# A two-layer attention and expert trunk on one core: the last norms behind the branch, four loads set apart, column sums by a product

## The chip, the core and the metric

The kernel runs on one core of a Trainium2 chip. The metric is the device time of one execution in microseconds. Five engines work side by side, each with its own queue of instructions that it takes in order: PE (TensorE, the matmuls), DVE (VectorE), ACT (ScalarE), POOL (GpSimd) and SP (SyncE, which issues nearly all loads). They wait for each other by semaphores.

## The reference

256 tokens of width 1024 go through two layers. Layer 0 mixes by multi-head latent attention (MLA), layer 1 by a sparse attention (DSA) with rotary keys, in which an indexer picks 64 keys for each query. After either mixer comes a PEER: eight heads, each with two sets of 128 keys, choose 16 of 16,384 experts for each token. Every sublayer ends in a norm. Cut to what matters here:

```
for i in range(2):
    m = _mla_mixer(x, ...) if i == 0 else _dsa_mixer(x, dsa_w_in, dsa_w_o)
    x = _layernorm(DN_ALPHA * x + m, ln_gain[i, 0], ln_bias[i, 0])
    f = _peer(x, peer_w_q[i], peer_sub_keys[i], peer_w_down[i], peer_w_up[i])
    x = _layernorm(DN_ALPHA * x + f, ln_gain[i, 1], ln_bias[i, 1])

def _peer(x, w_q, sub_keys, w_down, w_up):
    ...
    v1, i1 = lax.top_k(s1, 16)
    v2, i2 = lax.top_k(s2, 16)
    cand = (v1[..., :, None] + v2[..., None, :])          # 16 x 16 sums
    cand_idx = (i1[..., :, None] * 128 + i2[..., None, :])
    best, pos = lax.top_k(cand, 16)
    gate = softmax(best)
    a = einsum('td,ted->te', x, w_down[expert])
    y = einsum('te,ted->td', gelu(a) * gate, w_up[expert])
```

## The kernel before

**Number format.** PE multiplies in float16. Each f32 operand is split into two float16 parts, *hi* (ACT, line 88) and *lo* = value − hi (DVE, line 97; now and then POOL, lines 163 to 167, after ACT has scaled the raw block), and each product becomes three: hi·hi, hi·lo and lo·hi. Weights come in 512 KB blocks *raw* of 128 × 1024 (SP, line 132, six buffers), are split ahead of their use, and are multiplied by the tokens' parts *xh* and *xl*.

**The guard.** DVE's splits add up each lo as they go, one column of 128 partitions a split, in *sums*. At the end a judgement on these sums says whether float16 was safe: *fit* and *verdict* hold flags, `least` (line 559) squares the first 128 columns (*square*) and adds them over the partitions, `judge` (line 566) adds up the flags, and *sound* is their count. All engines load sound (line 1445) and compare it (line 1446); if a flag is missing, the whole computation is run a second time in a slower format (the fallback). Here it isn't: each engine goes past the fallback's code. `least` runs in the second PEER, whose code hands it to POOL between two of POOL's splits.

**The stages.** MLA, PEER, DSA, PEER. In the DSA, four pairs of query blocks (`heads(qT, h)`), then pairs of key blocks and the attention, head by head, and the output projection with w_o. Swapping halves for the rotation is two copies on ACT (lines 625 and 626), a product on POOL (627) and two operations on DVE (630 and 634); *s* are the scores. Four transfers of 512 KB for the norm behind the DSA (the layer's input x in two halves, gain and bias) are issued by SP in one go after the queries, lines 378, 611 and 612, ahead of the first w_o blocks.

A PEER has four parts: queries and scores; the down projection (products *d*, 64 steps of two key columns), during which the choice of experts is made; the placing of the gates (*gT*, *hot*, *place*, *G*); and the up projection (products *y*, 128 blocks). The choice (`choose`) is top-16 search on DVE (lines 1094 to 1098), then `pairs`: with the rank a of the first key only the first 16/(a + 1) of the second can be among the best 16, so 50 sums a head are made, in 16 adds on DVE (*cand*, line 1120) and 16 on POOL (*cell*, line 1123), for each of the two halves t of the tokens. The order in which the choice is mixed with the splits is set by a planner: each part yields its cost in ns, and `spend` takes as many parts as a step's income (PACE, 1420) pays for. Operations of one engine are then chained in this order.

`finish` ends a sublayer: the last four blocks of y for t = 0, then for t = 1, and the norms n0 and n1 (DVE lines 419 to 444, ACT 427, POOL 439). In the last layer it judges and stores the output (line 507); the branch comes behind it.

Of the kernel before, what the change touches and what calls it, by code (L numbers as in the profile page):

```python
# [10 lines left out]
F32 = mybir.dt.float32  # L11
# [4 lines left out]
ALU = mybir.AluOpType  # L16
# [23 lines left out]
OFF = [sum(SEG[:a]) for a in range(TOPK)]  # L40
CELLS = sum(SEG)
STAGGER = 4
PACE = 1420
# [21 lines left out]
BOTH, MOSTLY = 128, 704  # L65
CHECKS = 4 * P + BOTH

# [172 lines left out]
@with_exitstack  # L240
def tile_trunk(ctx: ExitStack, tc: tile.TileContext, ins, out: bass.AP, short, sound=None):
    nc = tc.nc
# [8 lines left out]
    rings = pool("rings", RING if short else 4)  # L251
    big = pool("big", 1)
    const = pool("const", 1)
# [3 lines left out]
    psp = pool("psp", 4, space=bass.MemoryType.PSUM)  # L257
    pyp = pool("pyp", 1, space=bass.MemoryType.PSUM)

# [6 lines left out]
    def py(i, name):  # L266
        return pyp.tile([P, 512], F32, tag=f"py{i}", name=name)
# [3 lines left out]
    fit = const.tile([P, 4], F32, tag="fit", name="fit")  # L271
    verdict = const.tile([1, 4 + BOTH], F32, tag="verdict", name="verdict")
    sound_rows = fit[:, 2:4]
    ones = lead.tile([P, 16], F32, tag="ones", name="ones")[:, 0:1]
    mhalf = lead.tile([P, 16], F32, tag="mhalf", name="mhalf")[:, 0:1]
    keep = [dram.tile([P, D], F32, tag=f"x{t}", name=f"x{t}") for t in range(2)]
# [7 lines left out]
    iotac = const.tile([P, CELLS, TOPK], F16, tag="iotac", name="iotac")  # L284
    arena = big.tile([P, 32768], F32, tag="arena", name="arena")
    A = arena.rearrange("p (b t) -> p b t", t=T)
# [11 lines left out]
    nc.vector.memset(mhalf, -0.5)  # L298

# [108 lines left out]
    class Norm:  # L408


        def __init__(self, queue, x, y2, g, b, r, z, sq):
            self.queue, self.x, self.y2, self.g, self.b, self.r, self.z, self.sq = queue, x, y2, g, b, r, z, sq
            self.st = small.tile([P, 6], F32, tag="st", name="st")

# [58 lines left out]
    def finish(y4, lhs_of, n, g, b, x, spare, lead=None):  # L473
# [21 lines left out]
        n0.result()  # L495
        if lead is None:
            if sound is not None:
                judge()
            n1.sums()
            n1.square()  # L500
            n1.centre()
            n1.scale()
            n1.result()
            for t in range(2):
                for h, q in enumerate((nc.sync, nc.scalar)):
                    s = slice(h * 512, (h + 1) * 512)
                    q.dma_start(out[t * P : (t + 1) * P, s], spare[t][:, s])
            return
        nc.sync.dma_start(keep[0], spare[0])
# [49 lines left out]
    def least():  # L559

        square = small.tile([P, BOTH], F32, tag="square", name="square", bufs=1)
        nc.gpsimd.tensor_tensor(square, split.cols[:, :BOTH], split.cols[:, :BOTH], op=ALU.mult)
        nc.gpsimd.tensor_reduce(square[0:1, :], square, axis=AX.C, op=ALU.add)
        nc.gpsimd.tensor_scalar(verdict[0:1, 4:], square[0:1, :], LEAST, None, op0=ALU.is_ge)

    def judge():

        assert not ws.late
        done = BOTH + split.n["most"]
        weigh_up(1, split.seen, done)  # L570
        nc.gpsimd.tensor_scalar(fit[:, 0:2], fit[:, 0:2], MOST * SMALL, None, op0=ALU.is_lt)  # L571
        nc.gpsimd.tensor_scalar(fit[:, 2:4], fit[:, 2:4], ROW, None, op0=ALU.is_ge)
        nc.gpsimd.tensor_reduce(verdict[0:1, 0:4], fit, axis=AX.C, op=ALU.add)
        nc.scalar.activation(verdict, verdict, AF.Copy, accum_out=fit[0:1, 0:1])
        nc.scalar.copy(sound, fit[0:1, 0:1])
# [358 lines left out]
    def dsa():  # L934
# [24 lines left out]
        proj(p[:72, :T], ws.get(), 72)  # L959
        xs, t1 = tmp()[:, 0, :], tmp()[:, 0, :]  # L960
        nc.scalar.copy(xs[0:32], p[32:64, :T])
        nc.scalar.copy(xs[32:64], p[0:32, :T])
# [3 lines left out]
        nc.scalar.copy(ki[64:128], ki[0:64])  # L966
        nc.scalar.mul(wT[64:72, :], p[64:72, :T], IDX_SCALE / unit)
        def weigh():
# [69 lines left out]
    def peer(li):  # L1038
# [74 lines left out]
        def pairs(t):  # L1113
            vh = v[t].rearrange("p (h two) k -> p h two k", two=2)
            dve(lambda: nc.vector.tensor_copy(idf[t], idx[t]))
            ih = idf[t].rearrange("p (h two) k -> p h two k", two=2)
            dve(lambda: nc.vector.tensor_scalar(ih[:, :, 0, :], ih[:, :, 0, :], float(NKEYS), None, op0=ALU.mult))
            for a in range(TOPK):
                w = slice(OFF[a], OFF[a] + SEG[a])
                dve(lambda: nc.vector.tensor_tensor(cand[t][:, :, w], vh[:, :, 1, 0 : SEG[a]],  # L1120
                                                    vh[:, :, 0, a : a + 1].to_broadcast([P, HEADS, SEG[a]]),
                                                    op=ALU.add))
                nc.gpsimd.tensor_tensor(cell[t][:, :, w], ih[:, :, 1, 0 : SEG[a]],
                                        ih[:, :, 0, a : a + 1].to_broadcast([P, HEADS, SEG[a]]), op=ALU.add)
# [162 lines left out]
        for k in range(NKEYS - STAGGER):  # L1287
            rows(y4, operand(k), ws.get(), k == 0, False)
            if k == 64:
                x = load_x(lnar, keep)  # L1290
                g, b = load_affine(lnar, li, 1)
                if last and sound is not None:
                    least()
# [3 lines left out]

        finish(y4, operand, NKEYS, g, b, x, spare, None if last else lead_values)

# [68 lines left out]
    dsa()  # L1368
    peer(1)

# [79 lines left out]
```

## Time and profile before

| | |
|---|---|
| median of 3 runs | 1746.27 us (1744.61 to 1748.59) |
| profiled execution, its own time | 1743.03 us |
| its span in the profile | 1741.7 us |
| mean granted TensorE clock | 0.994 |
| PE busy | 98% of the span |
| DVE, ACT, POOL busy | 78%, 63%, 24% |

In the profile a row of instructions gives the start and the duration in us, the engine, the line, the operation and what it writes and reads; behind it, in brackets, how long the engine had been idle and for whom it waited. A row of a window gives its ends and length, then each engine's busy time and count in the order PE, PEld (weight load), DVE, ACT, POOL, and then the granted TensorE clock, the share of the DMA engines and GB/s. A row of waits gives the total in us, how many times, and the longest. A row by line gives a count, the least, median and greatest duration in ns, and the first and last start.

### The profile page before, as it was taken

Reading aid. Unit: us, or ns where it says so; the run is one execution under the profiler, and the core shown is the slowest. Engines: PE = TensorE matmul, PEld = TensorE weight load, DVE = VectorE, ACT = ScalarE, POOL = GpSimd, SP = SyncE. Lnnn points to the kernel's source line nnn. Section 1 sums busy time; section 2 is a strip of 40 time slices with the busy share of each in tenths; the row PEclk is TensorE's granted clock in tenths of the full one; section 3 lists DMA queues with packets and bytes.
Section 4 is the critical chain, followed back from the end, with each engine's and each line's share of the span. In section 5 each row is a group of like instructions: output and inputs, shape, how many; then the busy total and the mean of one; then the engine's idle time right before and its main releaser. Section 6 shows DMA issues by size and latency. Waiting matters only on the chain.

```text
span 1741.7 us, 33230 instructions
## 1 busy us (share of the span) xinstructions
PE 1706.2 (98%) x12495; PEld 1195.2 (69%) x12495; DVE 1358.8 (78%) x3067; ACT 1095.5 (63%) x1905; POOL 418.8 (24%) x294
## 2 busy tenths in 40 slices
PE   9999999999999999999998999999999999999996
PEld 7678888999974444444676688889999944444443
DVE  7679999899986666665777899998899966666664
ACT  7665755888875455554667656567888855455552
POOL 3011354555530000000022143444555500000000
PEclk9999999999999999999999999999999999999999
DMA  9354556544466565555654435556444475565551
GB/s 343 139 182 170 206 182 212 207 174 172 170 211 225 204 206 201 203 202 204 222 190 159 169 145 188 196 198 219 171 171 176 174 245 205 204 205 203 200 204 50
DMA packets 93484, 335.62 MB, mean 193 GB/s; under 512 B 10368, under 2 KB 11392, under 8 KB 93312
## 3 DMA queue, kind: packets, MB, share of 16 engines
q1 hardware_dynamic: 93024, 332.87, 54.2%
q8 instruction: 100, 1.64, 0.4%
q14 instruction: 72, 0.59, 0.1%
q10 hardware_dynamic: 288, 0.52, 0.1%
HBM read 329.16 MB, written 4.19 MB: 191 GB/s over the span
## 4 chain that ended last, share of the span: by engine, by line
PE 78%; DVE 14%; issue 3%; DMA 2%; ACT 2%; POOL 1%; SPq 0%; POOLq 0%; DVEq 0%; ACTq 0%
PE y L341 40%; PE d L341 28%; DVE lo L97 6%; PE G L341 3%; DVE arena L1095 1%; DVE arena L1098 1%; DVE arena L1097 1%; PE qw L341 1%; DVE arena L1096 1%; ACT hi L88 1%; PE pq L341 1%; PE s L341 1%; DVE arena L1094 1%; PE q L341 1%; PE h L341 1%
## 5 line engine op out<-in xcount | busy, mean ns | idle before, releaser
L97 DVE SCALAR_TENSOR_TENSOR lo<-raw,hi 128x1024 f16<-128x1024 f32 (+1 forms) x571 | 784.0, 1377 | 229.5 <-ACT hi L88 228.6
L88 ACT ACTIVATE hi<-raw 128x1024 f16<-128x1024 f32 (+1 forms) x570 | 594.7, 1051 | 295.9 <-PE y L341 183.2
L341 PE MATMUL d<-xh,lo 128*128 128x256 f16 x2048 | 559.7, 273 | 8.1 <-DVE lo L97 5.7
L341 PE MATMUL d<-xh,hi 128*128 128x256 f16 x2048 | 560.0, 273 | 0.1
L341 PE MATMUL d<-xl,hi 128*128 128x256 f16 x2048 | 559.8, 273 | 0.0
L341 PEld LDWEIGHTS <-hi 128*128 128x128 f16 x5016 | 490.0, 98 | 60.2 <-issue 1.7
L341 PEld LDWEIGHTS <-xh 128*128 128x128 f16 x2320 | 226.4, 98 | 270.7 <-ACT xh L88 2.3
L341 PE MATMUL y<-lo,xh 128*128 128x512 f16 x1088 | 326.4, 379 | 0.0
L341 PE MATMUL y<-hi,xh 128*128 128x512 f16 x1088 | 326.0, 379 | 0.0
L341 PE MATMUL y<-hi,xl 128*128 128x512 f16 x1088 | 325.7, 379 | 0.0
L341 PEld LDWEIGHTS <-lo 128*128 128x128 f16 x2508 | 246.2, 98 | 40.8 <-DVE lo L97 8.4
L1218 POOL TENSOR_TENSOR gate<-hot,gate 128x512 f16<-128x512 f16 x128 | 219.8, 1736 | 191.6 <-DVE hot L1216 191.6
L341 PEld LDWEIGHTS <-xl 128*128 128x128 f16 x1160 | 113.3, 98 | 137.9 <-DVE xl L97 2.1
L1222 ACT ACTIVATE gate<-hot,rest 128x128 f16<-128x128 f16 x512 | 166.1, 413 | 5.3 <-DVE hot L1216 5.3
L88 ACT ACTIVATE xh<-arena 128x512 f16<-128x512 f32 x131 | 82.1, 629 | 133.3 <-PE y L341 132.3
L97 DVE SCALAR_TENSOR_TENSOR xl<-arena,xh 128x512 f16<-128x512 f32 x134 | 91.7, 687 | 60.4 <-ACT xh L88 60.2
L439 POOL TENSOR_TENSOR st<-st,mhalf 128x1 f32<-128x1 f32 x8 | 4.4, 555 | 422.0 <-DVE st L437 422.0
L167 POOL TENSOR_TENSOR lo<-raw,hi 128x1024 f16<-128x1024 f32 x26 | 58.7, 2260 | 175.1 <-ACT hi L165 141.5
L163 ACT ACTIVATE raw<-raw 128x1024 f32<-128x1024 f32 x26 | 27.5, 1056 | 112.2 <-DMA raw<-in_down 69.9
L1140 POOL TENSOR_TENSOR arena<-arena 128x800 f32<-128x800 f16 x32 | 73.9, 2308 | 77.0 <-DVE arena L1137 70.5
L1216 DVE TENSOR_TENSOR hot<-iota,place 128x1024 f16<-128x1024 f16 x128 | 82.8, 688 | 7.8 <-PE G L341 5.3
L571 POOL TENSOR_SCALAR fit<-fit 128x2 f32<-128x2 f32 x1 | 0.2, 228 | 326.3 <-DVE junk L556 326.3
(201 smaller groups left out, 1601.6 us busy)
## 6 DMA issues: line engine op xcount, KB each, us to landing
raw<-in_down SPq DMA_DIRECT2D x256, 512.0 KB, 3.3
raw<-in_up SPq DMA_DIRECT2D x256, 512.0 KB, 4.3
raw<-in_peer_q SPq DMA_DIRECT2D x24, 512.0 KB, 4.4
raw<-in_dsa_qk SPq DMA_DIRECT2D x16, 512.0 KB, 4.1
raw<-in_mla_w_o SPq DMA_DIRECT2D x8, 512.0 KB, 4.9
arena<-in_peer_q SPq DMA_DIRECT2D x8, 512.0 KB, 4.6
raw<-in_dsa_v SPq DMA_DIRECT2D x8, 512.0 KB, 4.5
raw<-in_dsa_w_o SPq DMA_DIRECT2D x8, 512.0 KB, 5.9
```

Of the source, the lines that this page charges most:

```text
L88: return nc.scalar.copy(o, src) if unit == 1.0 else nc.scalar.mul(o, src, unit)
L97: return nc.vector.scalar_tensor_tensor(o, src, unit, hi, op0=ALU.mult, op1=ALU.subtract, accum_out=total)
L163: self.act(lambda: nc.scalar.mul(raw, raw, unit))
L167: nc.gpsimd.tensor_tensor(lo, raw, hi if short else hi.bitcast(F32), op=ALU.subtract)
L341: return pe(lambda: nc.tensor.matmul(o, l, r, start=start, stop=stop, skip_group_check=True))
L1094: dve(lambda: nc.vector.max(vals[:, 0:8], src))
L1095: dve(lambda: nc.vector.max_index(ids[:, 0:8], vals[:, 0:8], src))
L1096: dve(lambda: nc.vector.match_replace(buf, vals[:, 0:8], src, GONE))
L1140: nc.gpsimd.tensor_tensor(o.rearrange("p k c -> p c k"), same, cell[t][:, h, :, None].to_broadcast([P, CELLS, TOPK]), op=ALU.mult)
L1216: nc.vector.tensor_tensor(hot, iota4[:, None].to_broadcast([P, 2, P, 4]), place16[:, :, None, four].to_broadcast([P, 2, P, 4]), op=ALU.is_ ...
L1218: nc.gpsimd.tensor_tensor(gate[:, 0], hot[:, 1].rearrange("p c j -> p j c"), gate16[:, four, None].to_broadcast([P, 4, P]), op=ALU.mult)
L1222: nc.scalar.mul(gate[:, 1, j, :], hot[:, 1, :, j], rest[:, t : t + 1])
```

## The change

1. `finish` for the last layer no longer makes the norms and the stores; it judges and returns a function `close` that makes them. The program calls it in the else arm of the condition, the fallback standing in the other arm. The pools that both arms need (the y banks, the arena, sound, mhalf, st) are made outside. The true arm, the fallback, stands straight behind the compare; the false arm stands behind it, and then the end of the program.
2. The DSA's four transfers are issued one at a time, each after one pair of query blocks.
3. `least` adds the squares over the partitions by one f32 product with a column of ones on PE, copies the 128 sums to a fifth column of fit on ACT, and compares there. A comparison of judge moves here too. verdict shrinks from 132 to 5 numbers, and the flags from 4 × 128 + 128 to 5 × 128.
4. `pairs` makes the sums of the ranks that have two partners in one add and those that have one in another: 7 adds on each engine for 16. It tells the planner 950 + 650 ns for 950 + 3 × 450.
5. In the DSA's `ki` a small scaling on ACT comes ahead of two copies.

```
-CHECKS = 4 * P + BOTH
+CHECKS = 5 * P
...
     def finish(y4, lhs_of, n, g, b, x, spare, lead=None):
...
-            norms.append(Norm(queue, x[t], y4[t], g, b, spare[t], spare[2 + t], spare[4]))
+            if lead is not None:
+                norms.append(Norm(queue, x[t], y4[t], g, b, spare[t], spare[2 + t], spare[4]))
+        if lead is None:
+            if short:
+                judge()
+
+            def close():
+                queue = queue_of()
+                for t in range(2):
+                    norm = Norm(queue, x[t], y4[t], g, b, spare[t], spare[2 + t], spare[4], shared["st"][t])
+                    norm.sums()
+                    norm.square()
+                    norm.centre()
+                    norm.scale()
+                    norm.result()
+                for t in range(2):
+                    for h, q in enumerate((nc.sync, nc.scalar)):
+                        s = slice(h * 512, (h + 1) * 512)
+                        q.dma_start(out[t * P : (t + 1) * P, s], spare[t][:, s])
+
+            return close
...
     def least():
         square = small.tile([P, BOTH], F32, tag="square", name="square", bufs=1)
+        p = ps("least")
         nc.gpsimd.tensor_tensor(square, split.cols[:, :BOTH], split.cols[:, :BOTH], op=ALU.mult)
-        nc.gpsimd.tensor_reduce(square[0:1, :], square, axis=AX.C, op=ALU.add)
-        nc.gpsimd.tensor_scalar(verdict[0:1, 4:], square[0:1, :], LEAST, None, op0=ALU.is_ge)
+        mm(p[:, 0:1], square, ones, True, True)
+        nc.scalar.copy(fit[:, 4:5], p[:, 0:1])
+        nc.gpsimd.tensor_scalar(fit[:, 4:5], fit[:, 4:5], LEAST, None, op0=ALU.is_ge)
+        nc.gpsimd.tensor_scalar(fit[:, 2:4], fit[:, 2:4], ROW, None, op0=ALU.is_ge)
...
+        x, g, b = [ar.take(D), ar.take(D)], ar.take(D), ar.take(D)
+        aside = [(x[0], keep[0]), (x[1], keep[1]), (g, ins["ln_gain"][1, 0].partition_broadcast(P)),
+                 (b, ins["ln_bias"][1, 0].partition_broadcast(P))]
         for h in range(0, HEADS, 2):
             turn_all(heads(qT, h))
+            with tc.issue_after(ws.last):
+                nc.sync.dma_start(*aside.pop(0))
         ws.share = 0
-        with tc.issue_after(ws.last):
-            x = load_x(ar, keep)
-            g, b = load_affine(ar, 1, 0)
...
-            for a in range(TOPK):
...
-                if a % 4 == 3:
-                    yield (950, 450, 450, 450)[a // 4]
...
+            for a in range(TWOS):
+                both(a, SEG[a], lambda i: i[:, :, 1, 0 : SEG[a]],
+                     lambda i: i[:, :, 0, a : a + 1].to_broadcast([P, HEADS, SEG[a]]))
+                if a == 3:
+                    yield 950
+            n = ONES - TWOS
+            both(TWOS, 2 * n, ...)
+            both(ONES, TOPK - ONES, ...)
+            yield 650
...
+        close = tile_trunk(tc, aps, o, True, shared)
+        count = nc.values_load(shared["sound"], min_val=0, max_val=CHECKS, ...)
+        with tc.If(count < CHECKS) as unsound:
+            tile_trunk(tc, aps, o, False, shared)()
+        with unsound.Else():
+            close()
```

How it moves instructions is shown at three places. First POOL in the second PEER, before; lo with raw and hi is a split:

```order
L167 TENSOR_TENSOR lo_11422<-raw_11218,hi_11421 128x1024 [waits PE_49,Activation_49,Pool_49]
L562 TENSOR_TENSOR square<-sums 128x128 [waits DVE_49]
L563 TENSOR_REDUCE square<-square 1x128 [waits Pool_49]
L167 TENSOR_TENSOR lo_11585<-raw_11387,hi_11584 128x1024 [waits PE_49,Activation_49]
L167 TENSOR_TENSOR lo_11748<-raw_11550,hi_11747 128x1024 [waits PE_49,Activation_49]
L564 TENSOR_SCALAR verdict<-square 1x128 [waits Pool_49]
```

and in the change:

```order
L168 TENSOR_TENSOR lo_11387<-raw_11183,hi_11386 128x1024 [waits PE_49,Activation_49,Pool_49]
L569 TENSOR_TENSOR square<-sums 128x128 [waits DVE_49]
L168 TENSOR_TENSOR lo_11550<-raw_11352,hi_11549 128x1024 [waits PE_49,Activation_49]
L168 TENSOR_TENSOR lo_11713<-raw_11515,hi_11712 128x1024 [waits PE_49,Activation_49,Pool_49]
L168 TENSOR_TENSOR lo_11859<-raw_11673,hi_11858 128x1024 [waits DVE_49,PE_49,Activation_49]
```

The reduction and the comparison behind it have gone from between the splits; the product that takes their place stands on PE at the end of d.

Then SP in the DSA, from the last blocks of queries and keys (in_dsa_qk) to the first of w_o, before (x is the layer's input, in two halves):

```order
L132 DMA raw_10268<-in_dsa_qk 128x1024 [waits Pool_49]
L132 DMA raw_10304<-in_dsa_qk 128x1024 [waits DMAHW7_49,DVE_49]
L132 DMA raw_10335<-in_dsa_qk 128x1024 [waits DMAHW6_49,DMAHW0_49,DVE_49]
L132 DMA raw_10372<-in_dsa_qk 128x1024 [waits Pool_49]
L132 DMA raw_10402<-in_dsa_qk 128x1024 [waits DMAHW2_49,DVE_49]
L378 DMA arena<-x_97 128x1024 [waits DMAHW1_49,PE_49]
L378 DMA arena<-x_98 128x1024 [waits PE_49]
L611 DMA arena<-in_ln_gain 128x1024 [waits DMAHW3_49,PE_49]
L612 DMA arena<-in_ln_bias 128x1024 [waits DMAHW4_49]
L132 DMA raw_10442<-in_dsa_w_o 128x1024 [waits DMAHW5_49,DVE_49]
L132 DMA raw_10473<-in_dsa_w_o 128x1024 [waits DMAHW6_49,DVE_49]
```

and in the change:

```order
L1032 DMA arena<-x_98 128x1024 [waits PE_49]
L133 DMA raw_10204<-in_dsa_qk 128x1024 [waits DMAHW5_49,DVE_49]
L133 DMA raw_10234<-in_dsa_qk 128x1024 [waits Pool_49]
L1032 DMA arena<-x_99 128x1024 [waits DMAHW6_49,PE_49]
L133 DMA raw_10271<-in_dsa_qk 128x1024 [waits DMAHW7_49,DVE_49]
L133 DMA raw_10302<-in_dsa_qk 128x1024 [waits DMAHW0_49,DVE_49]
L1032 DMA arena<-in_ln_gain 128x1024 [waits DMAHW1_49,PE_49]
L133 DMA raw_10340<-in_dsa_qk 128x1024 [waits DMAHW2_49,Pool_49]
L133 DMA raw_10370<-in_dsa_qk 128x1024 [waits DMAHW3_49,DVE_49]
L1032 DMA arena<-in_ln_bias 128x1024 [waits DMAHW4_49]
L133 DMA raw_10407<-in_dsa_w_o 128x1024 [waits DMAHW5_49,DVE_49]
L133 DMA raw_10438<-in_dsa_w_o 128x1024 [waits DMAHW6_49,DVE_49]
```

Three of the four transfers have moved ahead by six, four and two blocks of in_dsa_qk, and one alone still stands before w_o.

Last, ACT at the same place. raw_10473 is the second w_o block, which POOL splits, and q_10437 the first pair of key blocks, before:

```order
L88 ACTIVATE hi_10505<-raw_10335 128x1024 [waits DMAHW6_49,PE_49]
L625 COPY arena<-q_10366 64x512 [waits DVE_49,PE_49]
L626 COPY arena<-q_10366 64x512 [waits Activation_49]
L88 ACTIVATE hi_10535<-raw_10372 128x1024 [waits DMAHW7_49,PE_49]
L163 ACTIVATE raw_10473<-raw_10473 128x1024 [waits DMAHW6_49,DVE_49]
L88 ACTIVATE hi_10599<-raw_10402 128x1024 [waits DMAHW0_49,PE_49]
L625 COPY arena<-q_10437 64x512 [waits DVE_49,PE_49]
L626 COPY arena<-q_10437 64x512 [waits Activation_49]
```

and in the change, where they are raw_10438 and q_10402:

```order
L89 ACTIVATE hi_10433<-raw_10271 128x1024 [waits DMAHW7_49,PE_49]
L164 ACTIVATE raw_10438<-raw_10438 128x1024 [waits DMAHW6_49,DVE_49]
L89 ACTIVATE hi_10470<-raw_10302 128x1024 [waits DMAHW0_49,PE_49]
L633 COPY arena<-q_10334 64x512 [waits PE_49,Pool_49]
L634 COPY arena<-q_10334 64x512
L89 ACTIVATE hi_10500<-raw_10340 128x1024 [waits DMAHW2_49,PE_49]
L89 ACTIVATE hi_10564<-raw_10370 128x1024 [waits DMAHW3_49,PE_49]
L633 COPY arena<-q_10402 64x512 [waits DVE_49,PE_49]
L634 COPY arena<-q_10402 64x512 [waits Activation_49]
```

The scaling of the second w_o block has moved ahead of two hi and a pair of copies.

More of the change, by code (lines that the diff above doesn't have):

```diff
@@ L240, in tile_trunk @@
 @with_exitstack
-def tile_trunk(ctx: ExitStack, tc: tile.TileContext, ins, out: bass.AP, short, sound=None):
+def tile_trunk(ctx: ExitStack, tc: tile.TileContext, ins, out: bass.AP, short, shared):
     nc = tc.nc
@@ L257, in tile_trunk @@
     psp = pool("psp", 4, space=bass.MemoryType.PSUM)
-    pyp = pool("pyp", 1, space=bass.MemoryType.PSUM)
+    pyp, arena, mhalf, sound = shared["pyp"], shared["arena"], shared["mhalf"], shared["sound"]
     def oh_tile(tag, dt=F32):
@@ L408, in tile_trunk, with __init__ @@
     class Norm:
[L411 removed]
+        def __init__(self, queue, x, y2, g, b, r, z, sq, st=None):
             self.queue, self.x, self.y2, self.g, self.b, self.r, self.z, self.sq = queue, x, y2, g, b, r, z, sq
[L413 removed]
+            self.st = small.tile([P, 6], F32, tag="st", name="st") if st is None else st
         def sums(self):
@@ L495, in finish @@
         n0.result()
[L496 to L508, printed above, removed]
         nc.sync.dma_start(keep[0], spare[0])
@@ L1117, in pairs, with both @@
             dve(lambda: nc.vector.tensor_scalar(ih[:, :, 0, :], ih[:, :, 0, :], float(NKEYS), None, op0=ALU.mult))
-            for a in range(TOPK):
[L1119 to L1124, printed above, removed]
-                if a % 4 == 3:
-                    yield (950, 450, 450, 450)[a // 4]
+            def both(w, n, first, second):
+                k = OFF[w]
+                for engine, o, i in ((nc.vector, cand[t], vh), (nc.gpsimd, cell[t], ih)):
+                    o, f, g = o[:, :, k : k + n], first(i), second(i)
+                    if len(f.shape) == 4:
+                        o = o.rearrange("p h (a b) -> p h a b", b=f.shape[3])
+                    if engine is nc.vector:
+                        dve(lambda: engine.tensor_tensor(o, f, g, op=ALU.add))
+                    else:
+                        engine.tensor_tensor(o, f, g, op=ALU.add)
+            for a in range(TWOS):
[4 more added lines that the diff above has]
+            n = ONES - TWOS
+            both(TWOS, 2 * n, lambda i: i[:, :, 1, None, 0:2].to_broadcast([P, HEADS, n, 2]),
+                 lambda i: i[:, :, 0, TWOS:ONES, None].to_broadcast([P, HEADS, n, 2]))
+            both(ONES, TOPK - ONES, lambda i: i[:, :, 0, ONES:TOPK],
+                 lambda i: i[:, :, 1, 0:1].to_broadcast([P, HEADS, TOPK - ONES]))
+            yield 650
             for h in range(HEADS):
@@ L1291, in peer @@
                 g, b = load_affine(lnar, li, 1)
-                if last and sound is not None:
+                if last and short:
                     least()
@@ L1296, in peer @@
         spare = [lnar.take(D) for _ in range(5)]
-        finish(y4, operand, NKEYS, g, b, x, spare, None if last else lead_values)
+        return finish(y4, operand, NKEYS, g, b, x, spare, None if last else lead_values)
     xt = Arena(arena, 30720).take(NC, T)
@@ L1368, in tile_trunk @@
     dsa()
-    peer(1)
+    return peer(1)
 def _blocks(w):
@@ L1440 @@
     o = nc.dram_tensor("out_y", (T, D), F32, kind="ExternalOutput").ap()
-    with tile.TileContext(nc, schedule_with_timeline_sim=True) as tc:
-        with tc.tile_pool(name="sound", bufs=1) as pool:
-            sound = pool.tile([1, 1], mybir.dt.int32, tag="sound", name="sound")
-            tile_trunk(tc, aps, o, True, sound)
-            count = nc.values_load(sound, min_val=0, max_val=CHECKS, skip_runtime_bounds_check_because="it counts CHECKS flags")
-            with tc.If(count < CHECKS, preferred_fallthrough_block=False):
-                tile_trunk(tc, aps, o, False)
+    with tile.TileContext(nc, schedule_with_timeline_sim=True) as tc, ExitStack() as ctx:
+        held = ctx.enter_context(tc.tile_pool(name="held", bufs=1))
+        shared = {
+            "pyp": ctx.enter_context(tc.tile_pool(name="pyp", bufs=1, space=bass.MemoryType.PSUM)),
+            "banks": {},
+            "sound": held.tile([1, 1], mybir.dt.int32, tag="sound", name="sound"),
+            "st": [held.tile([P, 6], F32, tag=f"end{t}", name=f"end{t}") for t in range(2)],
+            "mhalf": held.tile([P, 16], F32, tag="mhalf", name="mhalf")[:, 0:1],
+            "arena": held.tile([P, 32768], F32, tag="arena", name="arena"),
+        }
+        nc.vector.memset(shared["mhalf"], -0.5)
+        close = tile_trunk(tc, aps, o, True, shared)
+        count = nc.values_load(shared["sound"], min_val=0, max_val=CHECKS,
+                               skip_runtime_bounds_check_because="it counts CHECKS flags")
+        with tc.If(count < CHECKS) as unsound:
+            tile_trunk(tc, aps, o, False, shared)()
+        with unsound.Else():
+            close()
     r = run_bass_kernel_spmd(nc, [arrays], core_ids=[0])
```

18 lines of the change are left out of this document (8 added, 10 removed).

## The prediction

> **What bounds the kernel now.** I read the page's head and chain first, then what PE waits for, then windows over the stages that the change touches.
>
> ```profile
> PE 1706.2 (98%) x12495; PEld 1195.2 (69%) x12495; DVE 1358.8 (78%) x3067; ACT 1095.5 (63%) x1905; POOL 418.8 (24%) x294
> PE 78%; DVE 14%; issue 3%; DMA 2%; ACT 2%; POOL 1%; SPq 0%; POOLq 0%; DVEq 0%; ACTq 0%
> PE s L341 <- DVE arena L634: 5.8, 1, 5.8
> PE d L341 <- DVE lo L97: 5.7, 4, 3.9
> 142.00:265.00 123.00, 122.79 (x1126) 109.92 (x1125) 116.10 (x411) 78.14 (x101) 44.99 (x48) 1.00 0.53 188
> 985.00:1140.00 155.00, 146.98 (x1316) 129.71 (x1314) 143.35 (x474) 89.39 (x118) 61.79 (x52) 0.99 0.46 167
> ```
>
> PE is the bound, and the change leaves its matmuls alone but for one. So it can only win where PE stands still or is clocked down, and after PE's last matmul. The two wait rows (total, times, longest) name the two places: one stall of 5.8 us at the DSA's first scores, and splits (lo) that come late in the second PEER. The two windows are the same stage, queries and choice, of the first PEER and the second: with DVE busy for 94% of it the first loses 0.21 us of PE, the second 8.02.
>
> **The lanes' reduction (L563).** What the second PEER has and the first has not:
>
> ```profile
> 1009.47 14.37 POOL L563 CROSS_LANE_REDUCE square<-square 128x128 f32<-128x128 f32 x1
> 1023.83 4.19 POOL L167 TENSOR_TENSOR lo<-raw,hi 128x1024 f16<-128x1024 f32 x2
> 1010.42 5.65 DVE L97 SCALAR_TENSOR_TENSOR lo<-raw,hi 128x1024 f16<-128x1024 f32 x1
> 1019.14 2.70 DVE L97 SCALAR_TENSOR_TENSOR lo<-raw,hi 128x1024 f16<-128x1024 f32 x1
> 1023.35 5.75 DVE L97 SCALAR_TENSOR_TENSOR lo<-raw,hi 128x1024 f16<-128x1024 f32 x1
> 1030.62 1.21 DVE L97 SCALAR_TENSOR_TENSOR lo<-raw,hi 128x1024 f16<-128x1024 f32 x1
> 1025.00:1030.00 5.00, 1.10 (x11) 0.75 (x9) 4.94 (x7) 0.00 (x0) 4.50 (x3) 1.00 0.00 0
> 1030.00:1035.00 5.00, 5.00 (x33) 3.85 (x31) 4.75 (x22) 0.00 (x0) 0.00 (x0) 0.66 0.69 253
> 1035.00:1040.00 5.00, 5.00 (x48) 4.49 (x46) 4.06 (x18) 4.75 (x7) 0.00 (x0) 1.00 0.27 81
> 1140.00:1145.00 5.00, 5.00 (x36) 4.01 (x34) 4.84 (x19) 4.21 (x7) 2.13 (x1) 0.74 0.83 315
> ```
>
> While POOL reduces, and then makes the two splits that stood behind it, three splits of DVE take 14.1 us where three at 1.21 take 3.63: 10.5 us of DVE gone. PE then has nothing for 3.90 us of 1025:1030, and runs at a granted clock of 0.66 in the next 5 us (33 matmuls, where 48 go at full clock: 1.56 us lost). DVE, at 92% in this stage, hardly makes that up. The remaining waits of the stage follow, and a second clocked stretch (36 of 48, 1.25 us) behind them.
>
> The edit takes L563 and L564 away and gives POOL two small operations on 128 partitions instead. If the backlog is the cause of all stalls of this stage, 8.02 + 1.56 + 1.25 = 10.8 us go, less what the first PEER loses at the same rate (0.21/123 × 155 = 0.3): **−10.5**. If only the stall straight behind it goes, −(3.90 + 1.56) = −5.5. I take −10.5: the first PEER is the nearest measurement, being the same code without the reduction.
>
> **The sums of pairs, 16 to 7 on each engine, twice in a PEER.**
>
> ```profile
> 1078.95 3.17 DVE L1120 TENSOR_TENSOR arena<-arena 128x128 f32<-128x128 f32 x16
> 1132.74 3.22 POOL L1123 TENSOR_TENSOR arena<-arena 128x128 f32<-128x128 f32 x16 [3.54 <-DVE arena L1117]
> 1135.91 2.13 POOL L167 TENSOR_TENSOR lo<-raw,hi 128x1024 f16<-128x1024 f32 x1
> 1135.00:1140.00 5.00, 2.70 (x20) 1.79 (x19) 4.79 (x21) 5.00 (x8) 3.04 (x7) 0.92 0.00 0
> ```
>
> Nine of 16 adds less are 9/16 × 3.2 = 1.8 us of each engine, four times. On DVE that is cover, not path, once the backlog is gone: 0. On POOL it brings the split at 1135.91 forward, for which PE stood 2.30 us; that stall is counted above already. With the reduction gone the adds' saving makes sure of it; so this part is at 0 beside the −10.5, and −2.3 without it. The lower charge of the planner moves the choice ahead against the splits, but by the order no split of DVE in either PEER gets more DVE work in front of it than it had, since nine adds have gone: 0, bounds ±1.
>
> **The product in place of the reduction.** One f32 matmul with its load stands where the second PEER turns from d to y.
>
> ```profile
> L341 PEld LDWEIGHTS ms<-ones,arena x8: 190/192/193, 27.8 to 36.8; 128*128 128x128 f32 x8
> L341 PE MATMUL ms<-ones,arena x8: 169/250/251, 27.9 to 36.8; 128*128 128x1 f32 x8
> ```
>
> The same shape costs 0.25 us, 0.44 with its load uncovered: **+0.3**. Its operand is ready long before. The copy on ACT lies beside PE: 0.
>
> **The four loads of the DSA.**
>
> ```profile
> 904.68 1.06 ACT L88 ACTIVATE hi<-raw 128x1024 f16<-128x1024 f32 x1 [0.35 <-PE q L341]
> 913.12 1.06 ACT L163 ACTIVATE raw<-raw 128x1024 f32<-128x1024 f32 x1 [7.38 <-DMA raw<-in_dsa_w_o]
> 915.75 0.58 ACT L626 COPY arena<-q 64x512 f32<-64x512 f32 x1
> 916.40 1.27 POOL L627 TENSOR_TENSOR arena<-arena 128x512 f32<-128x512 f32 x1 [10.02 <-ACT arena L626]
> 917.70 0.69 DVE L634 TENSOR_TENSOR arena<-arena 128x512 f32<-128x512 f32 x1 [0.66 <-POOL arena L627]
> 905.28 0.33 SPq L132 DMA_DIRECT2D raw<-in_dsa_w_o  x1
> raw<-in_dsa_w_o SPq DMA_DIRECT2D x4, 512.0 KB, 6.8
> raw<-in_dsa_qk SPq DMA_DIRECT2D x3, 512.0 KB, 3.6
> 915.00:920.00 5.00, 1.55 (x5) 1.37 (x6) 2.99 (x5) 4.87 (x8) 1.65 (x2) 0.74 0.00 0
> 920.00:925.00 5.00, 5.00 (x27) 3.68 (x26) 4.93 (x16) 2.70 (x9) 3.89 (x2) 0.58 0.57 211
> ```
>
> The scores wait for the first keys: ACT's swap copies, POOL, DVE in a chain, and ACT stood in front of them until the second w_o block had landed. Four loads of 512 KB ahead of it made it take 6.8 us instead of the 3.6 of a dsa_qk block. Spread out they are done sooner: on SP each now stands between two dsa_qk loads, where SP waits for buffers anyway; an issue takes 0.33 us like the one shown, and what the loads overwrite has been free since the first layer: 0 for what is queued behind them. It is still issued at 905.28 (by the lo that frees its buffer), so by the 3.6 it lands about 908.9 instead of 912 to 913. But in the new order ACT meets it two blocks earlier, and ahead of the keys' copies stand, from 908.9: the scaling 1.06, three hi of 1.05, two pairs of copies of 1.2, together 6.6, so 915.5. Before, the copies ended at 916.33: **−0.8**. A landing at 3.1 us would make it −1.3, one as late as before 0 to +2.4. The clock stays at 0.58 to 0.74 for two stretches here, so it takes a shorter stall to save one of them: the windows give 1.7 us for it at most, which I keep for the range.
>
> The Trainium skill's page "TensorE: Matmul & The Clock Gate" (Part 1, "What's actually happening") has full clock return after one busy window of 3.4 us in a grid that runs free of the kernel. The trace's first slow window holds 1.1 us of idle, so its second slow one agrees; by that rule a chance shift of the grid alone could make this part −2.5.
>
> **The end.** Norms and stores behind the branch instead of ahead of it:
>
> ```profile
> 1716.93 0.19 ACT L575 CAST sound<-fit 1x1 int32<-1x1 f32 x1
> 1722.41 0.69 DVE L419 SCALAR_TENSOR_TENSOR arena<-arena,y 128x512 f32<-128x512 f32 x1 [7.03 <-PE y L341]
> 1727.59 0.69 DVE L419 SCALAR_TENSOR_TENSOR arena<-arena,y 128x512 f32<-128x512 f32 x1
> L1445 DVEq TENSOR_LOAD <-sound x1: 541/541/541, 1731.4 to 1731.4; - x1
> L1446 DVEq COMPARE_BRANCH  x2: 51/58/65, 1732.0 to 1732.9; - x2
> L1441 DVEq DRAIN  x2: 10/34/58, 1736.6 to 1740.3; - x2
> L1446 SPq COMPARE_BRANCH  x2: 38/46/53, 1733.1 to 1736.7; - x2
> L1441 SPq EVENT_SEMAPHORE  x10: 17/28/28, 1739.4 to 1741.6; - x10
> ```
>
> Now SP waits for the last store to land (1736.7), takes the branch over the fallback, and goes on at 1739.4: 2.7 us on the path. In the change each engine branches as soon as sound is written, and the end lies straight behind the arm. So these 2.7 go, **−2.7** (2.5 to 3.2 with the semaphore checks that follow). The price is a jump ahead of the norms: on DVE 3.65 us (1732.95 to 1736.6). From sound at 1717.12 come the load, 0.54, the compare, 0.06, and the jump: 1721.4. DVE isn't wanted before 1722.41, so 1.0 us is left over. n1's sums (1727.59) begin without idle time behind n0, so each microsecond of excess would be lost whole. SP, ACT and POOL are wanted only after DVE's first sums.
>
> **Sum.** −10.5 + 0.3 − 0.8 − 2.7 = −13.7. The profiled execution took 1743.03 us (a span of 1741.7), which is 0.19% under the median of the runs, 1746.27; on that median it makes 1732.6, and I say **1732**.
>
> **Rivals.**
> - *Only the stall straight behind the reduction goes.* DVE at 92% of the stage is for it, the first PEER at 94% without a stall is against it. −5.5 + 0.3 − 0.8 − 2.7 = −8.7: 1737.5. Chance 0.16.
> - *The jump doesn't fit into DVE's wait.* The arm's code has to be brought in twice, say at a block border: another 3.7 (DVE's own jump). n0 then begins at 1725.1, 2.7 late, and the end gains nothing: 1735. For it speaks that the jumps in the trace take some 50 times their compares; against it the 1 us left. Chance 0.12. The Trainium skill's page "Runtime: NRT & Kernel Launch" (Instruction fetch mechanics) says that a taken branch out of a window of two pages fetches the target's page before it goes on; the jumps of 2.5 to 3.65 us agree, and no run here shows a second fetch.
> - *Slower: the choice, drawn forward by the lower charge, crowds out the splits in both PEERs.* DVE's lead there is worth about 6.6 us (10.5 lost, 3.90 felt by PE); if more work than that comes before a split, the first PEER too pays 10.8 and the second keeps its own: +10.8 + 0.3 − 0.8 − 2.7 = +7.6, 1754. Against it stands the order. Chance 0.04.
> - *The work that the reduction hid was not the backlog's cause, and the end's wait comes back elsewhere*, so that no part shows: within 0.2% (about 3.5 us, what the runs can tell). Chance 0.05.
>
> The forecast itself (1728 to 1734) has 0.63. The range takes in the first two rivals, and below the clock's 1.7 and the DSA's 0.5: 1726 to 1740. Faster 0.91, same 0.05, slower 0.04.
>
> **What would show it.** No POOL row of 14 us at 1009, DVE's splits there at 1.2, PE busy for over 154 of 155 us in that stage, and a granted clock of 1.00 from 1030 to 1150. L163 of the second w_o block runs about 909, the scores start about 917.6. DVE's first sums of the end start when y is ready, no more than 0.1 after it, and SP's last wait runs straight into the end. I am wrong if PE stalls for lo still near 1080 and 1135 of the old time, if DVE reaches the arm later than y, or if ACT's early wait for w_o starves the splits behind it.

## The result, and the profile after

The changed kernel takes 1729.91 us (median of 4 runs, 1728.14 to 1732.27) against 1746.13: a ratio of 0.9907, with a 95% interval of 0.9889 to 0.9924. That is 16.2 us less, where 14 were forecast. Its profiled execution took 1731.02 us, with a span of 1729.1. One execution of run 1 below took 2221.39 us at a granted clock of 0.753; it stands in that run's median, not in its ratio.

First the same views as before: the page's head and chain, PE's waits, and the windows over the two PEERs' queries and choice, moved with the work (1.5 us later in the first, 3 us later in the second).

```profile
PE 1702.9 (98%) x12497; PEld 1193.2 (69%) x12497; DVE 1346.9 (78%) x3033; ACT 1096.5 (63%) x1908; POOL 393.5 (23%) x257
PE 86%; DVE 7%; issue 3%; ACT 2%; DMA 1%; POOL 1%; DVEq 0%; SPq 0%; POOLq 0%; ACTq 0%
PE s L340 <- DVE arena L642: 4.6, 1, 4.6
PE d L340 <- DVE lo L98: 2.4, 3, 1.0
PE G L340 <- POOL gate L1242: 1.8, 4, 0.5
143.50:266.50 123.00, 120.86 (x1102) 107.28 (x1101) 115.67 (x393) 75.39 (x99) 39.74 (x30) 1.00 0.54 181
988.00:1143.00 155.00, 154.12 (x1406) 137.72 (x1404) 139.20 (x505) 96.83 (x127) 45.51 (x33) 1.00 0.56 182
1028.00:1033.00 5.00, 5.00 (x49) 4.49 (x47) 4.72 (x22) 4.97 (x9) 0.00 (x0) 1.00 0.46 161
1138.00:1143.00 5.00, 4.99 (x46) 4.24 (x45) 4.79 (x21) 4.58 (x6) 0.36 (x1) 1.00 0.52 184
```

DVE has halved its share of the chain, from 14% to 7%. The second PEER loses 0.88 us of PE where it lost 8.02, and both stretches of half clock there are gone (the granted clock is 1.00 from 1030 to 1150). But the first PEER, which lost 0.21, now loses 2.14, and the scores' stall is down by only 1.2 us. New are the waits of G for POOL's gates: two in each PEER, 1.8 us together.

Since PE does the same matmuls in both, the trace can be cut at the first matmul of each kind. The table gives the us from cut to cut; the last column is the range over the profiles of other kernels below whose code in that stage is the changed kernel's.

| stage | before | after | other profiles |
|---|---|---|---|
| first PEER, first d to first y | 365.66 | 369.39 | 366.9 to 368.1 |
| DSA, first q to first scores | 37.46 | 36.22 | 36.2 to 37.7 |
| scores to the second PEER's queries | 55.05 | 53.99 | 53.9 to 55.8 |
| second PEER, first d to first y | 377.98 | 368.40 | 366.6 to 368.6 |
| last y to the end of the span | 13.84 | 7.96 | 7.9 to 8.0 |

All other stages agree within 0.6 us, or 1 at the start. Ahead of the first d these add up to 1.5 us, by which profiles of one code differ there too (142.4 to 143.9). On the means of these profiles the change is worth about +1.9 in the first PEER (367.7 against 365.8), −1 in the DSA, −10.1 in the second PEER (367.9), and −5.6 at the end (two more profiles with the end as before have 13.3 and 13.5). That makes −14.8, inside the interval of the ratio (−13 to −19). So the sum of the forecast holds, and several of its terms do not.

At the place of the reduction, POOL and the splits of DVE:

```profile
1012.08 0.40 POOL L569 TENSOR_TENSOR square<-sums 128x128 f32<-128x128 f32 x1 [12.45 <-PE pq L340]
1012.43 2.13 POOL L168 TENSOR_TENSOR lo<-raw,hi 128x1024 f16<-128x1024 f32 x1
1021.92 2.71 POOL L168 TENSOR_TENSOR lo<-raw,hi 128x1024 f16<-128x1024 f32 x1 [7.36 <-ACT hi L166]
L98 DVE SCALAR_TENSOR_TENSOR lo<-raw,hi x8: 1204/1206/2144, 1010.8 to 1035.8; 128x1024 f16<-128x1024 f32 x8
```

POOL goes straight on to its split, and the eight splits of DVE from 1011 to 1036 have a median of 1.21 us; only those beside a split of POOL take longer (2.14).

The DSA, ACT's and POOL's rows ahead of the scores and the DMA rows of w_o from 895 to 915:

```profile
913.89 1.06 ACT L164 ACTIVATE raw<-raw 128x1024 f32<-128x1024 f32 x1 [8.15 <-DMA raw<-in_dsa_w_o]
915.92 0.58 ACT L633 COPY arena<-q 64x512 f32<-64x512 f32 x1
919.75 0.58 ACT L634 COPY arena<-q 64x512 f32<-64x512 f32 x1
920.41 1.27 POOL L635 TENSOR_TENSOR arena<-arena 128x512 f32<-128x512 f32 x1 [1.96 <-ACT arena L634]
raw<-in_dsa_w_o SPq DMA_DIRECT2D x3, 512.0 KB, 3.6
```

The second w_o block now lands about 4 us after its issue. Yet ACT waits longer for it, 8.15 us for 7.38, as it comes to it earlier; behind it stand a hi, the copies at 915.92, two more hi and only then the keys' copies, ending at 920.33. First q is at 886.24 here and at 880.99 before, so the copies end 34.1 us after it where they ended after 35.3.

The end, ACT's sound, DVE's first sums, the branch, SP's checks, and the stores:

```profile
1710.30 0.19 ACT L583 CAST sound<-fit 1x1 int32<-1x1 f32 x1
1715.85 0.69 DVE L418 SCALAR_TENSOR_TENSOR arena<-arena,y 128x512 f32<-128x512 f32 x1 [7.09 <-PE y L340]
L1479 DVEq COMPARE_BRANCH  x1: 76/76/76, 1711.1 to 1711.1; - x1
L1479 SPq COMPARE_BRANCH  x1: 54/54/54, 1711.1 to 1711.1; - x1
L1465 SPq EVENT_SEMAPHORE  x12: 17/28/28, 1714.3 to 1729.1; - x12
DMA to landing us min/median/max: 2.0/2.1/2.4
```

The jump fits: DVE starts when y is ready, 5.34 us ahead of the last matmul's start as against 5.41. The stores land in 2.0 to 2.4 us. In the kernel before the same row, and the instruction fetches from the first store to the end (packets, MB, share), read:

```profile
DMA to landing us min/median/max: 2.1/3.0/3.9
q14 instruction: 8, 0.07, 1.4%
q8 instruction: 2, 0.03, 1.1%
```

and in the changed kernel, whose jumps lie ahead of the stores, but for PE's, the fetches are:

```profile
q8 instruction: 2, 0.03, 1.3%
```

### The profile page after: what moved, and what is told of

It reads as the page before. It is cut to its first block, busy times and chain, and to the rows that moved or that the text cites. A ratio compares the mean times of both kernels' runs of the same rounds, so it can differ in the third digit from the quotient of the medians.

```text
span 1729.1 us, 33166 instructions
## 1 busy us (share of the span) xinstructions
PE 1702.9 (98%) x12497; PEld 1193.2 (69%) x12497; DVE 1346.9 (78%) x3033; ACT 1096.5 (63%) x1908; POOL 393.5 (23%) x257
## 4 chain that ended last, share of the span: by engine, by line
PE 86%; DVE 7%; issue 3%; ACT 2%; DMA 1%; POOL 1%; DVEq 0%; SPq 0%; POOLq 0%; ACTq 0%
PE y L340 40%; PE d L340 33%; PE G L340 3%; DVE lo L98 2%; PE pq L340 2%; PE qw L340 1%; ACT hi L89 1%; PE v L340 1%; PE s L340 1%; PE o L340 1%; PE h L340 1%; DMA raw<-in_down 1%; PE ps L340 1%; PE q L340 1%; PE qi L340 1%
## 5 line engine op out<-in xcount | busy, mean ns | idle before, releaser
L98 DVE SCALAR_TENSOR_TENSOR lo<-raw,hi 128x1024 f16<-128x1024 f32 (+1 forms) x571 | 776.1, 1363 | 234.4 <-ACT hi L89 233.4
```

What stands on the lines that cost most here:

```text
L98: return nc.vector.scalar_tensor_tensor(o, src, unit, hi, op0=ALU.mult, op1=ALU.subtract, accum_out=total)
```

## The experiments

Each is the changed kernel (*after*) or the kernel before with one edit. Times are medians; ratios are to the kernel before on the same chip, with their intervals. Runs 1 to 4, 5 to 8 and 9 to 12 were made on three different chips, so across these groups the ratios compare better than the times. Stages are read from the profile as in the table.

**1. The planner's charge as before.**

```
-            yield 650
+            yield 1350
```

> The changed kernel, with pairs charged at 950 + 1350 ns as before instead of 950 + 650; its seven adds stay. Theory A (the lower charge packs the choice too densely between the splits): the first PEER's extra stalls, about 3.7 us in the profile after, go, and some of the 4 us of the second PEER's choice; the first y of layer 0 starts about 3.7 us earlier, total about 1725. Theory B (the choice's stalls come from where POOL's splits and adds fall against DVE's, not from the charge): PE loses as much in other places, total within 1.5 us of 1729.9.

1727.0 us, ratio 0.9899 (0.9879 to 0.9919). The first PEER's stage is 365.58, 3.8 less than in the profile after; the second's is 367.94. The time alone can't tell this from the changed kernel (0.9907). The stage says Theory A for the first PEER. In the second the charge trades one stall for another: there is no wait for POOL's gates at G in this run, but in the second PEER PE waits for the split behind POOL's adds, which it doesn't in the profile after:

```profile
PE d L340 <- POOL lo L168: 1.8, 1, 1.8
```

**2. The reduction back on POOL, all else changed.**

```
-        mm(p[:, 0:1], square, ones, True, True)
-        nc.scalar.copy(fit[:, 4:5], p[:, 0:1])
+        nc.gpsimd.tensor_reduce(square[0:1, :], square, axis=AX.C, op=ALU.add)
+        nc.gpsimd.tensor_scalar(verdict[0:1, 4:], square[0:1, :], LEAST, None, op0=ALU.is_ge)
...
```

> The changed kernel with the reduction over the lanes back on POOL. Theory A (DVE's backlog from the reduction is the cause of all the second PEER's stalls): the second PEER loses 10 us again, though the seven adds give back up to 2 of them, total 1738 to 1740. Rival (only the stall straight behind the reduction hangs on it, the rest was the sixteen adds): 5.5 us, total about 1735.5.

1736.64 us, ratio 0.9953 (0.9937 to 0.997). POOL's rows and PE's wait are back:

```profile
1012.48 14.37 POOL L569 CROSS_LANE_REDUCE square<-square 128x128 f32<-128x128 f32 x1
1026.84 4.19 POOL L168 TENSOR_TENSOR lo<-raw,hi 128x1024 f16<-128x1024 f32 x2
PE d L340 <- DVE lo L98: 6.7, 4, 4.2
1025.00:1035.00 10.00, 5.82 (x42) 4.45 (x40) 9.79 (x21) 0.00 (x0) 7.51 (x4) 0.86 0.33 106
```

The second PEER's stage is 374.90: 7.0 more than the mean without the reduction. 4.2 us is the stall straight behind it, 1.4 the clock (0.86 over these 10 us), the rest smaller stalls after. So the figure lies between the two theories, and the seven adds with their charge have taken 3.1 us off the stage (377.98 before).

**3. Norms and stores ahead of the branch again.**

```
-        close = tile_trunk(tc, aps, o, True, shared)
+        tile_trunk(tc, aps, o, True, shared)()
...
-        with tc.If(count < CHECKS) as unsound:
-            tile_trunk(tc, aps, o, False, shared)()
-        with unsound.Else():
-            close()
+        with tc.If(count < CHECKS, preferred_fallthrough_block=False):
+            tile_trunk(tc, aps, o, False, shared)()
```

> The changed kernel with the two norms and the stores ahead of the branch again. As predicted (only the jump of SP lies on the path): +2.7 us, 1732.6. Rival from the two traces (the jumps' code is fetched while the last stores land, 3.9 us instead of 2.1, and the last barrier is longer too): +5.5 to 6, about 1735.5, with the last store's landing again near 3.9 us after its issue.

1736.01 us, ratio 0.9954 (0.9937 to 0.997). From the last y to the end it takes 12.87 us, 4.91 more than after. The stores' landing, the instruction fetches from the first store on, SP's branch and its first step behind it:

```profile
DMA to landing us min/median/max: 2.0/2.9/3.8
q14 instruction: 8, 0.07, 1.3%
q8 instruction: 2, 0.03, 1.1%
L1479 SPq COMPARE_BRANCH  x2: 38/46/53, 1723.8 to 1727.3; - x2
L1465 SPq EVENT_SEMAPHORE  x10: 17/28/28, 1730.0 to 1731.3; - x10
```

2.66 us is SP's jump, 1.7 the last store's landing (3.8 for 2.0 to 2.1), 0.5 the eight semaphore checks behind the jump, which in the changed kernel run while SP waits for the landing. The rival is right on the size, without a longer last barrier, and the fetch can be followed packet by packet: one of 16 KB, 1.5 us long, starts 0.14 us after the last store is issued. Over the 56 stores of the fourteen profiles of this study, each of the 11 that had a fetch of 16 KB start within 1.2 us after its issue took 3.4 to 4.5 us; two more of those that had one start at 1.5 to 2.1 us took 4.0 and 4.2, and all others 2.0 to 2.4. In runs 1, 2, 6, 10 and 11 it hit the store before, beside PE's jump, off the path. No run took the fetch away and left all else, so that the fetch is the cause is argued from these 56 stores, not shown by an edit.

**4. The second w_o block split by ACT and DVE.**

```
-            return heads(kT, h, ahead=(3, 2), pooled=True)
+            return heads(kT, h, ahead=(3, 2))
```

> The changed kernel, but the second w_o block of the DSA is split by ACT and DVE instead of ACT and POOL, so that no scaling of it stands in ACT's queue ahead of the first keys' copies. Theory A (ACT's early wait for this block, 8.15 us in the profile after, is what the scores wait for): the stall of 4.6 us ahead of the first scores falls under 1 us and the half clock behind it goes, -5 to -6 us, about 1724.5. Rival (the scores wait for the keys' blocks themselves, or DVE is late with one more split): within 1.5 us of 1729.9.

1720.64 us, ratio 0.9868 (0.9851 to 0.9884). First q to scores is 31.45 us where it was 36.22, and the scores' stall is no longer among PE's waits. The keys' last copy, the window before the scores and the scores:

```profile
911.63 0.58 ACT L634 COPY arena<-q 64x512 f32<-64x512 f32 x1
910.00:915.00 5.00, 5.00 (x49) 4.49 (x47) 3.83 (x8) 3.22 (x4) 1.28 (x1) 1.00 0.34 118
915.09 1.26 PE L340 MATMUL s<-arena 128*128 128x128 f32 x7
```

PE goes from q to s without a pause, at full clock. Theory A holds: a scaling in ACT's queue, for a block that nobody needed yet, was what the scores had been waiting for; run 10 shows the same with the loads together, as they are before the change. The gain is larger than expected. By the ratios it is some 7 us: in the three profiles without this stall (runs 4, 6 and 10) the stage is 5.3 us shorter than on the mean of the changed kernel's code (36.8), and the next one, to the second PEER's queries, 2.6 us shorter (52.3 for 54.9), as no half clock follows.

**5. The changed kernel as a control.**

> The changed kernel once more, beside the others of this call on one chip. By every theory the ratio of 0.991 to the kernel before, about 1728 to 1730, and the first PEER's d stage (first d to first y) between 366.9 and 369.4 us, as in the four profiles with this code so far.

1729.71 us, ratio 0.9911 (0.9895 to 0.9926); the first PEER's stage is 367.07, the second's 367.58, first q to scores 37.27. So the first profile after (369.39) was at the upper end for the first PEER, and the part of it that is the change's is nearer 2 us than 4.

**6. Edits 1 and 4 together.**

> Both edits together on the changed kernel: the second w_o block split by ACT and DVE, and the charge of pairs at 950 + 1350. Theory A (the lower charge costs the first PEER 2.4 us on the mean of the profiles): 2 to 3 us under the unpooled version, about 9 us under the changed kernel, ratio to before about 0.9855, first d to first y 365.6. Theory B (the difference between those profiles is chance): the same as the unpooled version, ratio 0.987, first d to first y 367 to 369.

1719.01 us, ratio 0.9851 (0.9835 to 0.9868). The first PEER's stage is 365.33. In four profiles with the old charge and either number of adds (runs 1 and 6, the kernel before, run 8) it is 365.3 to 366.0; in nine with the new charge and seven adds it is 366.6 to 369.4 (run 12 among them). That is Theory A, at 2 us. But the second PEER's stage is 370.22, 2.4 above the mean: run 1's stall behind POOL's adds is there, with 3.4 us of half clock behind it (1.7 us lost), which run 1 hasn't:

```profile
PE d L340 <- POOL lo L168: 1.8, 1, 1.8
1117.05 1.80 POOL L1138 TENSOR_TENSOR arena<-arena 128x128 f32<-128x128 f32 x7 [3.54 <-PE d L340]
1119.79 2.12 POOL L168 TENSOR_TENSOR lo<-raw,hi 128x1024 f16<-128x1024 f32 x1 [0.93 <-PE d L340]
```

In the total it is not told apart from run 4, so the 2 to 3 us expected don't show there. It is the fastest median of all kernels here, and the intervals of both versions' ratios lie below those of the changed kernel (0.9907, and 0.9911 in run 5).

**7. The four loads together again.** load_x and load_affine behind the loop, as before.

> The changed kernel with the four loads of the DSA issued together again, ahead of w_o. As predicted (the loads held up the second w_o block, which held up the scores): the block lands 3 us later after its issue, 6.8 instead of 4.0, the scores start 0.8 us to 3 us later, since ACT now meets the block two blocks earlier. Rival (ACT's order alone sets it): last q before the scores within 0.5 us, 36.2 from the first q to the scores. Total +0 to +3 us, by the profile's stage.

1728.71 us, ratio 0.991 (0.9891 to 0.9929); first q to scores 36.0. ACT's order has gone back with the loads, and the block lands later:

```profile
906.81 1.06 ACT L89 ACTIVATE hi<-raw 128x1024 f16<-128x1024 f32 x1 [0.35 <-PE q L340]
913.79 1.06 ACT L164 ACTIVATE raw<-raw 128x1024 f32<-128x1024 f32 x1 [5.92 <-DMA raw<-in_dsa_w_o]
916.42 0.58 ACT L634 COPY arena<-q 64x512 f32<-64x512 f32 x1
```

Counted from the first q (883.14 here, 886.24 after) the second w_o block is issued at the same time, 23.6 us, and ACT has it at 30.7 instead of 27.7: the burst does hold it up by 3 us. But in this order only a hi and the keys' own copies stand behind the scaling, 3.2 us to the end of the copies, where it is 6.4 with spread loads. One cancels the other, and no gain from the spreading shows. The rival's result, though not by its reason.

**8. The kernel before with the product alone.** The edit of `least` and `judge`.

> The kernel before with one part of the change: column sums by the product instead of the reduction. Theory A (DVE's backlog from the reduction makes all the later stalls): the second PEER's d stage falls from 378.0 to 367.7 us, total -10, about 1736. Rival (the pairs' saving is needed for the later stalls at 1070 to 1142): the stage falls by about 6 to 7, to 371 to 372, total about 1739.5.

1737.75 us, ratio 0.9957 (0.9943 to 0.9972). The second PEER's stage is 370.61: −7.4, a little over the rival's 6 to 7, well short of Theory A's 10, and the counterpart of run 2's 7.0. What stays is the stall behind POOL's adds, and two waits for splits of DVE:

```profile
PE d L341 <- POOL lo L167: 2.7, 2, 2.2
PE d L341 <- DVE lo L97: 1.8, 2, 1.4
1127.93 3.26 POOL L1125 TENSOR_TENSOR arena<-arena 128x128 f32<-128x128 f32 x16 [3.54 <-DVE arena L1119]
1131.15 2.13 POOL L167 TENSOR_TENSOR lo<-raw,hi 128x1024 f16<-128x1024 f32 x1
```

**9. Sixteen adds on DVE, seven on POOL**, at the changed charge.

```
-                for engine, o, i in ((nc.vector, cand[t], vh), (nc.gpsimd, cell[t], ih)):
+                for engine, o, i in ((nc.gpsimd, cell[t], ih),):
...
+            for a in range(TOPK):
+                dve(lambda: nc.vector.tensor_tensor(cand[t][:, :, w], ...))
...
```

> The changed kernel, but DVE makes the pairs' sums in sixteen adds again, POOL in seven; the charge stays at 950 + 650. The second PEER's d stage is 377.98 us before, 370.6 with the product alone and 367.6 on the mean of the profiles with both. Theory A (of the 3 us between them, POOL's split behind POOL's adds is the cause, as the 2.3 us wait at 1135 before suggests): it stays at 367 to 368.5. Theory B (DVE's nine adds, 1.8 us twice, are the cause, since DVE is behind): it goes up to 370 to 371. Total +0 or +3.

1737.55 us, ratio 0.9966 (0.9954 to 0.9979): some 8 us more than after, or 10 by the ratios. The second PEER's stage is 372.69 (+4.8), the first's 371.38 (+3.7). Theory B has the sign and is short of the size. The profile shows why; DVE's adds and POOL's split beside them in the first PEER, and the adds' durations there:

```profile
193.57 4.67 DVE L1142 TENSOR_TENSOR arena<-arena 128x128 f32<-128x128 f32 x16
195.51 2.12 POOL L168 TENSOR_TENSOR lo<-raw,hi 128x1024 f16<-128x1024 f32 x1
L1142 DVE TENSOR_TENSOR arena<-arena x32: 161/229/2159, 193.6 to 253.0; 128x8 f32<-128x8 f32 x16, 128x16 f32<-128x16 f32 x6, 128x128 f32<-128x128 f32 x2, 128x64 f32<-128x64 f32 x2
```

POOL, done sooner with its seven adds, begins a split while DVE still adds, and one small add of DVE takes 2.16 us (2159 ns in the last row) instead of some 0.2; in two more of the four groups of sixteen adds one takes 2.11. So the run isn't a clean test of DVE's nine adds: it adds a collision to them. It does show that DVE has no such time to spare here, for what PE waits for are DVE's splits (7.7 us in nine waits, 2.4 in three after). In the first PEER before, with sixteen adds on either engine and the old charge, it had: PE lost 0.21 us.

**10. Run 4 with the loads together.**

> The changed kernel with the second w_o block split by ACT and DVE and the four loads issued together again. If the scores wait for that block only through ACT's queue, the placing of the loads is worth nothing once it is out of the way: first q to scores 31.4 to 32 us, total as with spread loads, ratio to before about 0.987. Rival (the burst also delays what the keys need): first q to scores 33 to 35, +2 to +3 us.

1720.74 us, ratio 0.9865 (0.9849 to 0.9882); first q to scores 31.45, as in run 4. Where the loads stand makes no difference in this form either.

**11. The DSA quite as before** (the loads together, ki's scaling behind its copies).

> The changed kernel with the loads together and the small scaling in ki behind the two copies again, so the DSA is as it was before. With the loads together and the new ki the way from the first q to the scores took 36.0 us, before the change 37.3 to 37.5. If the scaling's place makes that difference: 37.3 to 37.5. If chance does: 36.0 to 36.7.

1729.92 us (two executions), ratio 0.9917 (0.9897 to 0.9937); first q to scores 37.74. That would fit the scaling's place, but the changed kernel's own code had 36.16 to 37.73 in six profiles, and the DSA as before 37.28 to 38.78 in three. Inconclusive: the ranges overlap, and chance covers it.

**12. The kernel before with the seven adds alone**, at their charge.

> The kernel before with the seven adds and their charge of 950 + 650 alone. If the parts add up (product -7.4, seven adds -3.1 in the second PEER; the charge +2.0 in the first): the second PEER's d stage at 374.9 us, first PEER's at 367.7, total -1, within the noise. If the adds matter only where the reduction is gone: 378 in the second PEER, total +2.

1742.39 us, ratio 0.9987 (0.9977 to 0.9996). Second PEER 374.71, first 366.55: the parts add up, with the first PEER's loss at the low end (+0.7).

## Why the prediction was right, and where it wasn't

The time, 1729.91, lies 2 us under the 1732 forecast. By its steps:

- **The reduction, −10.5.** The place, the price of DVE's lost time and the clock were right. The step that failed is that the backlog made *all* stalls of the stage: the product alone brought 7.4 (run 8), its removal from the changed kernel cost 7.0 (run 2). That is neither the −10.5 nor the rival's −5.5. The first PEER was no full measurement of the second without the reduction, since POOL's split behind the sixteen adds stalled PE by 2.1 us in the second and 0.2 in the first. The product's +0.3 holds: its two passes take 0.28 us on PE.
- **The seven adds, 0 beside the reduction's term.** With their charge they brought 3.1 to 3.3 us in the second PEER with the reduction in place (runs 2 and 12), and 2.7 without it (run 8's 370.61 against 367.9). The text had a stall behind POOL's adds, at 2.30 us, and counted it as the reduction's. It is 2.1 to 2.2 us in the second PEER with sixteen adds and the old charge (before, run 8), still 1.8 with seven adds and the old charge (runs 1 and 6), and gone wherever the charge is lower: so it takes the charge to remove it. What seven adds took away at the old charge are waits for DVE's splits, 1.8 us in run 8 and none in run 1 (0.65 in run 6). By these profiles, one or two of a kind, the step that failed is that DVE's share of the adds was cover, not path. Reduction, product and adds together made −10.1, for −10.2 in the sum: the forecast is right there because the change holds both parts, not because it had told them apart.
- **The lower charge, 0 with bounds of ±1.** It cost the first PEER about 2 us. In the nine profiles with the new charge and seven adds PE waits 0.8 us there for POOL's gates ahead of G, in the four with the old charge not at all; in eight of the nine a split of DVE is late by 0.3 to 1.0 us some 110 us after the first d. The second PEER has 0.8 to 1.0 us of the same wait at G, against the stall that the charge removes. The order did show fewer operations of DVE ahead of each split; why gates and splits make PE wait all the same, no run shows. The rival with this mechanism was right on its direction in the first PEER, at a fifth of its price.
- **The loads, −0.8.** The landing came about as forecast (4.0 us after the issue for 3.6), and so did ACT's order behind it. But the gain attributed to the pair of them isn't theirs: with the loads together the stage takes 36.0, not more (run 7). The mean over the changed kernel's code (36.8 in six profiles) is 1 us under that of the code before (37.8 in three), and its cause stays open between ki's scaling and chance. The stall itself was there to be taken, for 5 us more and 2.6 of half clock behind it (run 4).
- **The end, −2.7.** It is −5.6. The jump was right to 0.1 us, and DVE's wait held it. The step that failed is that SP's jump was all there was on the path: the last store's landing, 3.8 to 3.9 us, was taken as the store's own time, and 1.7 us of it came with the fetch beside it; the checks behind the jump, 0.5, had been in the bounds. The profile before has its last barrier longer by 0.9 besides (runs 8 and 12, with the same end, by 0.7 and 0.8), which run 3 hasn't, and which is left unexplained.
- **The jump's rival** didn't come: DVE was not late. The Trainium skill's page "Runtime: NRT & Kernel Launch" (Instruction fetch mechanics) has a taken branch out of its two-page window wait until the target's page is fetched. SP's 2.66 us and DVE's 3.65 a jump in the rows shown agree.
- **The clock's grid.** The Trainium skill's page "TensorE: Matmul & The Clock Gate" (Part 1) has it free-running. The traces agree: with the same code two profiles had one half-clock window behind the scores (the first after, and run 3: 53.99 and 53.92 us from the scores to the next PEER's queries) and four had two (runs 1, 2, 5 and 9: 54.2 to 55.8). The records of the clock show what decides it: in the two, the scores began 0.5 and 0.0 us into the first slow window of 3.4 us; in all nine profiles here with two windows, 0.8 to 3.1 us into it. So up to 1.9 us in that stage is chance, as allowed for in the range.

So +1.9 in the first PEER, which was not foreseen, and 2.9 more at the end largely cancel. That the time came out within 2 us of the forecast is luck to that extent; the stages of the two large gains were foreseen, but only half the size of the second.

## What to carry to other kernels

When one operation seems to cause a chain of stalls, look at what releases each of them: those that another engine ends will stay. A transfer that lands sooner helps only if nothing in front of the waiting work is moved with it; ask for whom the waiting instruction waits, and whether its result is needed yet: taking it out of the queue was worth some 7 us here, where no placing of the transfers showed a gain. Branch while an engine has nothing to do, and not while the last stores are under way.

## What the runs showed of the hardware

A store of 256 KB lands 3.4 to 4.5 us after its issue when a fetch of 16 KB of code starts within 1.2 us after it, and 2.0 to 2.1 when none is near. And an add of DVE on 128 x 8 or 128 x 16 elements, 0.16 to 0.34 us otherwise in that row of adds, took 2.16 in run 9 when it met POOL's split of 128 x 1024, which took 2.12: they start at the same 195.51, and DVE is through when POOL is. Two more such adds in that run took 2.11.
